# First projection of an encoder kernel: the order of casts and low parts against the latents, set by hand

## The chip, the cores and the metric

The kernel runs on 1 core of one Trainium2 chip. The metric is the device time of one execution in microseconds (us): a median over several runs of the same program. A profiled execution gives a trace beside it.

## The reference, cut to what matters

The reference is a two-layer encoder over 1024 rows of width 1024 in float32. Layer 0 mixes tokens by latent attention, layer 1 by differential attention; each layer then has a SwiGLU block, and a layer norm follows each of these parts. The change lies in the very first step of layer 0, in which the input is projected to three pieces and two of them are normalised:

```python
h = x @ w_in                                      # (1024, 1024) @ (1024, 704)
c_q, c_kv, k_rope = jnp.split(h, [384, 640], axis=-1)
c_q = _rmsnorm(c_q, g_q)                          # 384 columns
c_kv = _rmsnorm(c_kv, g_kv)                       # 256 columns
k_rope = _apply_rope(k_rope, cos, sin)            # 64 columns
```

where `_rmsnorm(x, g)` is `x * rsqrt(mean(x * x) + eps) * g` over the columns. The 704 columns that result are called the latents here. The queries, keys and values of all heads are made from them.

## The kernel before, in words

**Products in three parts.** Every float32 operand of a matmul is split into a high part, which is the operand rounded by a cast on ACT (ScalarE), and a low part, which is operand minus high part, made on DVE (VectorE) or POOL (GpSimd). A product is then three matmuls: high x high, high x low and low x high.

**The first projection.** The 1024 rows are worked on in eight row blocks of 128 (tb = 0 to 7). For each of them:

- `load_x` (line 1067) has SP (SyncE) load the block's transposed input into tile `x` (1076), ACT casts it into `xh` (1077), and DVE makes the low part `xl` (1078). There are two buffers for `x` and three each for `xh` and `xl`. So block tb's cast takes the buffer of block tb - 3, and has to wait until the last matmul that reads that block's `xh` has been done; in the same way for `xl`. Blocks 0 and 1 are loaded and cast in two pieces each.
- `project` (1111) runs 8 x 3 x 2 = 48 matmuls: for each of eight slices of 128 input columns and each of the three parts, one into PSUM tile `hq` (384 columns, line 1121) and one into `hk` (320 columns, line 1122). Blocks 0 and 1 are projected together, since the weights `wih`, `wil` are still arriving then. There are three PSUM banks for `hq` and three for `hk`, so block 3 takes those of block 0.
- `latents` (1125) makes the normalised rows `cn`: two sums of squares on ACT (lines 1128 and 1129, each an activation and a read of its accumulator), two small steps on DVE that make the variance `cve` (1131, 1132), a power on POOL that makes the scale `crs` (1134), five small DVE steps for the rotary columns (1138 to 1142), and two DVE steps that scale `hq` (1143) and `hk` (1144) into `cn`.
- `turn_c` (1147) transposes `cn` on TensorE in six blocks of 128 x 128 into PSUM tile `cp` (recorded at line 148, in the helper `tr`). ACT casts the result (1154) and DVE makes its low part (1155).

The loop at the end of the stage goes over row blocks (0, 1), 2, 3 and so on up to 7: load this block, project it, transpose the latents of the block before, make this block's latents.

**Beside it** the weights of the stage arrive in eight slices (`wraw`, cast at line 136 into `wih`, low part at line 137 into `wil`), and so do the first weights of the attention that follows (`r_wa`, cast at line 136 into `h_wa`, low part on POOL at line 137 into `l_wa`).

**What sets the order.** Each engine carries out its own instructions in the order of its queue. The order is not the order of the program's text: a planner in the framework goes through the program with a model of how long each operation takes, and gives every engine what is ready in the model. Data dependences become semaphore waits. The helper `behind(i, j)` (155) adds a dependence without a semaphore: instruction `i` keeps its place behind `j` in the plan. It is used elsewhere in the kernel before; the first projection has none. `ends` is a dictionary in which such instructions are kept for later use.

Of the kernel before, what the change touches and what calls it, by code (L numbers as in the profile page):

```python
# [11 lines left out]
AF = mybir.ActivationFunctionType  # L12
ALU = mybir.AluOpType
# [29 lines left out]
def trunk(  # L43
# [33 lines left out]
    V, A, G, T = nc.vector, nc.scalar, nc.gpsimd, nc.tensor  # L77
# [29 lines left out]
    def f32(t):  # L107
        return t.bitcast(F32)
# [4 lines left out]
    def ps_s(name):  # L113
        return ps.tile([P, 512], F32, tag="s", bufs=ps_bufs[0], name=name)

    def ps_m(name):
        return ps.tile([P, 512], F32, tag="m", bufs=ps_bufs[1], name=name)

    def ps_t(name):
        return ps.tile([P, 512], F32, tag="t", bufs=ps_bufs[2], name=name)  # L120
# [4 lines left out]
    def small(name, n=1):  # L125
        return sp.tile([P, 2], F32, tag="small", name=name, bufs=22)[:, :n]

    def load_w(src, cols, name, hi=None, lo=None, eng=None, raw=None, ins=False):

        if raw is None:  # L130
            raw = wp.tile([P, 1024], F32, tag="wr", bufs=2, name=f"r_{name}")
        nc.sync.dma_start(raw[:, :cols], src)
        if hi is None:
            hi = wp.tile([P, 1024], F32R, tag="wh", name=f"h_{name}")
            lo = wp.tile([P, 1024], F32R, tag="wl", name=f"l_{name}")
        A.copy(hi[:, :cols], raw[:, :cols])
        j = (eng or G).tensor_tensor(lo[:, :cols], raw[:, :cols], f32(hi[:, :cols]), ALU.subtract)
        return (hi, j.ins) if ins else (hi, lo)
# [8 lines left out]
    def tr(ps_out, in_):  # L147
        T.transpose(ps_out, in_, ident)

    def bcast_row(pool, src, n, name, tag):  # L150
        t = pool.tile([P, n], F32, tag=tag, name=name, bufs=1)
        nc.gpsimd.dma_start(t, src.partition_broadcast(P))
        return t

    def behind(i, j):

        tc.add_manual_dep(
            i, j.name,
            mybir.DependencyInfo(mybir.DependencyClass.NoSync, mybir.DependencyReason.DATA),
            reason="kept in program order",  # L160
        )
# [46 lines left out]
    ends = {}  # L208
# [855 lines left out]
    with tc.tile_pool(name="a0", bufs=2, side="right") as pool:  # L1064
        xs, win = {}, []

        def load_x(tb, k0=0, k1=KD):

            if tb not in xs:
                xs[tb] = [  # L1070
                    pool.tile([P, D], dt, tag=tag, name=f"{tag}_{tb}", bufs=2 if tag == "x" else 3)
                    for dt, tag in ((F32, "x"), (F32R, "xh"), (F32R, "xl"))
                ]
            c = slice(k0 * P, k1 * P)
            xt, xh, xl = (t[:, c] for t in xs[tb])
            nc.sync.dma_start(xt, xt_in[tb, :, c])
            A.copy(xh, xt)
            V.tensor_tensor(xl, xt, f32(xh), ALU.subtract)

        def load_w_in(k, n=1):  # L1080
            hi = pool.tile([P, 704], F32R, tag=f"wih{k}", name=f"wih{k}", bufs=1)
            lo = pool.tile([P, 704], F32R, tag=f"wil{k}", name=f"wil{k}", bufs=1)
            raw = pool.tile([P, 704], F32, tag="wraw", name=f"wraw{k}", bufs=5)
            win.append((hi, lo))
            if n == 1:
                _, j = load_w(w_in_a[k], 704, f"win{k}", hi, lo, G if k > 2 and k % 2 else V, raw, True)
                return j
            for c in (slice(0, 384), slice(384, 704)):
                nc.sync.dma_start(raw[:, c], w_in_a[k][:, c])
                A.copy(hi[:, c], raw[:, c])  # L1090
                V.tensor_tensor(lo[:, c], raw[:, c], f32(hi[:, c]), ALU.subtract)


        load_x(0, 0, 2)
        load_w_in(0, 2)
        load_x(1, 0, 2)
        load_w_in(1)
        load_x(0, 2, 8)
        load_w_in(2)
        load_x(1, 2, 8)  # L1100
        third = load_w_in(3)
        for k in range(4, KD):
            load_w_in(k)
        nc.sync.dma_start(ident, c_ident)
        with tc.issue_after(third):
            kt = pool.tile([P, NTB, P], F32, tag="kt", name="kt", bufs=1)
            nc.gpsimd.dma_start(kt, c_krope)
            gq = bcast_row(pool, g_q, RQ, "gq", "gq")
            gk = bcast_row(pool, g_kv, RKV, "gk", "gk")

        def project(tbs):
            ms = [(ps_m(f"hq{tb}"), ps_t(f"hk{tb}")) for tb in tbs]
            for k in range(KD):
                kc = slice(k * P, (k + 1) * P)
                wh, wl = win[k]
                for tb, (hq, hk) in zip(tbs, ms):
                    _, xh, xl = xs[tb]
                    for lh, w, st, sp_ in (
                        (xh, wh, k == 0, False), (xh, wl, False, False), (xl, wh, False, k == KD - 1)
                    ):  # L1120
                        T.matmul(hq[:, :384], lh[:, kc], w[:, 0:384], start=st, stop=sp_)  # L1121
                        T.matmul(hk[:, :320], lh[:, kc], w[:, 384:704], start=st, stop=sp_)
            return ms

        def latents(tb, hq, hk):
            junk = pool.tile([P, 384], F32, tag="junk", name=f"junk{tb}")
            ssq = small(f"ssq{tb}", 2)
            A.activation(junk, hq[:, :384], AF.Square, accum_out=ssq[:, 0:1])
            A.activation(junk[:, :256], hk[:, :256], AF.Square, accum_out=ssq[:, 1:2])
            ve = small(f"cve{tb}", 2)  # L1130
            V.tensor_scalar(ve[:, 0:1], ssq[:, 0:1], 1.0 / RQ, RMS_EPS, ALU.mult, ALU.add)
            V.tensor_scalar(ve[:, 1:2], ssq[:, 1:2], 1.0 / RKV, RMS_EPS, ALU.mult, ALU.add)
            rs = small(f"crs{tb}", 2)
            G.tensor_tensor(rs, ve, mhalf, ALU.pow)
            cn = pool.tile([P, 768], F32, tag="cn", name=f"cn{tb}")
            ra = pool.tile([P, 64], F32, tag="ra", name=f"ra{tb}")
            rb = pool.tile([P, 64], F32, tag="rb", name=f"rb{tb}")
            V.tensor_tensor(ra, hk[:, 256:320], kt[:, tb, 0:64], ALU.mult)
            V.tensor_tensor(rb[:, 0:32], hk[:, 288:320], kt[:, tb, 64:96], ALU.mult)
            V.tensor_tensor(rb[:, 32:64], hk[:, 256:288], kt[:, tb, 96:128], ALU.mult)  # L1140
            V.tensor_tensor(cn[:, 640:704], ra, rb, ALU.add)
            V.tensor_tensor(cn[:, 704:768], ra, rb, ALU.add)
            V.scalar_tensor_tensor(cn[:, :384], hq[:, :384], rs[:, 0:1], gq, ALU.mult, ALU.mult)
            V.scalar_tensor_tensor(cn[:, 384:640], hk[:, :256], rs[:, 1:2], gk, ALU.mult, ALU.mult)
            return cn

        def turn_c(tb, cn):
            hf, c, tcs = tb // 4, slice((tb % 4) * P, (tb % 4) * P + P), slice(tb * P, tb * P + P)
            for k0, nk, dst in ((0, 4, [t[hf][:, :, c] for t in lat4]), (4, 2, [t[:, :, tcs] for t in lat2])):
                pc = ps_s(f"cp{tb}_{k0}")  # L1150
                for k in range(nk):
                    tr(pc[:, k * P:(k + 1) * P], cn[:, (k0 + k) * P:(k0 + k + 1) * P])
                src = pc[:, :nk * P].rearrange("p (k t) -> p k t", k=nk)
                A.copy(dst[0], src)
                V.tensor_tensor(dst[1], src, f32(dst[0]), ALU.subtract)

        done = []
        for tbs in ((0, 1), (2,), (3,), (4,), (5,), (6,), (7,)):
            for tb in tbs:
                if tb > 1:  # L1160
                    load_x(tb)
            ms = project(tbs)
            for tb, cn in done:
                turn_c(tb, cn)
            done = [(tb, latents(tb, *m)) for tb, m in zip(tbs, ms)]
        for tb, cn in done:
            turn_c(tb, cn)
# [177 lines left out]
    with ExitStack() as st:  # L1345
# [11 lines left out]
        for ql in q_lo:  # L1357
            for mp in range(2):
                b = slice(64 - mp * 64, 128 - mp * 64)
                z = bb[b, :512]  # L1360
                i = G.tensor_tensor(ql[b, mp * 512:mp * 512 + 512], z, z, ALU.subtract).ins
# [260 lines left out]
```

## Time and profile before

| | us |
|---|---|
| median of 3 runs | 2267.78 |
| lowest and highest of them | 2267.59, 2267.83 |
| the profiled execution's own time | 2268.24 |
| its span, from the first instruction to the last | 2266.5 |

In the lines of the profile PE is TensorE's matmuls and PEld its weight loads; DVE, ACT, POOL and SP are the engines named above, and a q behind the name is the engine's queue of DMA issues. A line of a timeline has the start in us from the beginning of the span, the length, the engine, the line of the kernel, the operation, the tile written and the tiles read, the shapes, and a count where neighbours are merged. Where the engine stood still ahead of it, square brackets give how long and what ended the wait. A line of the waits says who waited for whom: us in total, how often, and the longest. Buffer numbers are left out of the tiles' names, so `xl` is the low part of any row block. Matmuls overlap, so a matmul's length is more than the time between two starts.

### The profile page before, as it was taken

Reading aid. Unit: us, or ns where it says so; the run is one execution under the profiler, and the core shown is the slowest. Engines: PE = TensorE matmul, PEld = TensorE weight load, DVE = VectorE, ACT = ScalarE, POOL = GpSimd, SP = SyncE. Lnnn points to the kernel's source line nnn. Section 1 sums busy time; section 2 is a strip of 40 time slices with the busy share of each in tenths; the row PEclk is TensorE's granted clock in tenths of the full one; section 3 lists DMA queues with packets and bytes.
Section 4 is the critical chain, followed back from the end, with each engine's and each line's share of the span. In section 5 each row is a group of like instructions: output and inputs, shape, how many; then the busy total and the mean of one; then the engine's idle time right before and its main releaser. Section 6 shows DMA issues by size and latency. Waiting matters only on the chain.

```text
span 2266.5 us, 31066 instructions
## 1 busy us (share of the span) xinstructions
PE 2240.2 (99%) x11410; PEld 1912.8 (84%) x11410; DVE 1542.9 (68%) x2894; ACT 1014.3 (45%) x2097; POOL 773.9 (34%) x626
## 2 busy tenths in 40 slices
PE   8999999999999999999999999999999999999998
PEld 8999998888888888888888898878788888888886
DVE  5676765696766667767576667576686656668778
ACT  4365564352333334444465656564442333334444
POOL 3232341114444440455432424221114444430551
PEclk9999999999999999999999999999999999999999
DMA  5010125434435338454320212063334223238443
GB/s 203 11 37 31 42 70 186 143 127 151 174 130 204 114 129 327 183 192 158 98 52 22 68 34 64 21 223 126 125 138 163 90 103 107 100 112 324 165 180 150
DMA packets 105545, 287.76 MB, mean 127 GB/s; under 512 B 7968, under 2 KB 30112, under 8 KB 94896
## 3 DMA queue, kind: packets, MB, share of 16 engines
q1 hardware_dynamic: 101552, 277.44, 34.5%
q0 software_dynamic: 3840, 8.33, 1.4%
q8 instruction: 90, 1.47, 0.3%
q14 instruction: 63, 0.52, 0.1%
HBM read 204.47 MB, written 77.07 MB: 124 GB/s over the span
## 4 chain that ended last, share of the span: by engine, by line
PE 94%; DVE 2%; DMA 1%; issue 1%; ACT 1%; POOL 0%; SPq 0%; DVEq 0%; POOLq 0%; ACTq 0%
PE gb L548 15%; PE gc L548 10%; PE ga L548 10%; PE dw L872 7%; PE dx L872 5%; PE s_a L220 4%; PE zp_a L418 3%; PE s_b L220 3%; PE dv L872 3%; PE dy L872 3%; PE bp L145 3%; PE bp L143 3%; PE bp L144 3%; PE o_a L263 2%; PE o_b L263 2%; PE hq L1121 1%
## 5 line engine op out<-in xcount | busy, mean ns | idle before, releaser
L504 ACT CAST op_g<-gr 128x512 fp32r<-128x512 f32 x240 | 146.8, 621 | 376.9 <-PE gb L548 190.6
L505 POOL TENSOR_TENSOR op_g<-gr,op_g 128x512 fp32r<-128x512 f32 x104 | 145.5, 1404 | 255.3 <-ACT op_g L504 149.5
L505 DVE TENSOR_TENSOR op_h<-rh,op_h 128x512 fp32r<-128x512 f32 x152 | 140.7, 951 | 51.5 <-ACT op_h L504 51.5
L548 PE MATMUL ga<-xh_m,op_g 128*128 128x512 f32 x512 | 168.2, 389 | 0.0
L872 PE MATMUL dw<-op_w_t,op_h 128*128 128x512 f32 x660 | 151.1, 390 | 0.0
L504 ACT CAST op_h<-rh 128x512 fp32r<-128x512 f32 x152 | 91.9, 619 | 127.2 <-PE dx L872 35.0
L872 PEld LDWEIGHTS dw<-op_w_t,op_h 128*128 128x128 f32 x660 | 123.7, 188 | 25.6
L228 ACT ACTIVATE l_b<-l_b,mx_b 128x256 f32<-128x256 f32 (+7 forms) x128 | 99.4, 777 | 73.1 <-DVE mx_b L223 71.4
L505 POOL TENSOR_TENSOR op_w_b<-rw_b,op_w_b 128x512 fp32r<-128x512 f32 x44 | 64.4, 1488 | 172.9 <-ACT op_w_b L504 165.7
L505 DVE TENSOR_TENSOR op_g<-gr,op_g 128x512 fp32r<-128x512 f32 x136 | 111.7, 825 | 16.8 <-ACT op_g L504 16.4
L872 PE MATMUL dx<-op_w_b,op_h 128*128 128x512 f32 x528 | 121.5, 390 | 1.0 <-DVE op_w_b L505 1.0
L1426 POOL TENSOR_SCALAR l_b<-l_b,rb,cst 128x128 f32<-128x128 f32 (+3 forms) x64 | 52.5, 821 | 199.3 <-DVE rb L1425 187.9
L872 PEld LDWEIGHTS dx<-op_w_b,op_h 128*128 128x128 f32 x528 | 98.8, 188 | 23.0 <-DVE op_w_b L505 2.6
L548 PE MATMUL gb<-t3h_f,op_g 128*128 128x512 f32 x352 | 115.4, 389 | 1.4 <-DVE tmp L637 1.4
L548 PE MATMUL gb<-t2h_f,op_g 128*128 128x512 f32 x352 | 115.4, 390 | 0.4 <-DVE op_g L505 0.4
L548 PE MATMUL gc<-t1h_f,op_g 128*128 128x512 f32 x352 | 115.6, 389 | 0.0
L548 PE MATMUL gb<-t4h_f,op_g 128*128 128x512 f32 x352 | 115.5, 389 | 0.0
L548 PE MATMUL gc<-b22h_f,op_g 128*128 128x512 f32 x352 | 115.3, 389 | 0.0
L548 PEld LDWEIGHTS ga<-xh_m,op_g 128*128 128x128 f32 x512 | 96.1, 188 | 19.9
L505 POOL TENSOR_TENSOR op_g<-s,op_g 128x512 fp32r<-128x512 f32 x40 | 55.3, 1381 | 167.9 <-ACT op_g L504 159.8
L143 PE MATMUL bp<-xT_f,h_wb 128*128 128x512 f32 x256 | 101.7, 397 | 0.0
L144 PE MATMUL bp<-xT_f,h_wb 128*128 128x512 f32 x256 | 101.6, 397 | 0.0
(388 smaller groups left out, 6688.6 us busy)
## 6 DMA issues: line engine op xcount, KB each, us to landing
gr<-in_w_gu SPq DMA_DIRECT2D x44, 1024.0 KB, 6.9
rh<-h_dr SPq DMA_DIRECT2D x28, 1024.0 KB, 4.9
h_dr<-sh SPq DMA_DIRECT2D x22, 1024.0 KB, 4.9
h_dr<-hp SPq DMA_DIRECT2D x22, 768.0 KB, 4.2
tt<-in_w_dn SPq DMA_DIRECT2D x22, 512.0 KB, 7.6
rh<-h_dr SPq DMA_DIRECT2D x12, 768.0 KB, 4.4
wo_dr<-op_pwo SPq DMA_DIRECT2D x16, 512.0 KB, 3.5
z<-xs_dr SPq DMA_DIRECT2D x16, 512.0 KB, 11.5
```

The costliest lines, as they stand in the source:

```text
L143: T.matmul(ps_out, lh, rh, start=(i == 0), stop=False)
L144: T.matmul(ps_out, lh, rl, start=False, stop=False)
L145: T.matmul(ps_out, ll, rh, start=False, stop=(i == n - 1))
L220: T.matmul(s[:, :w], lh, rh[:, ks], start=(j == 0), stop=(j == len(q_pass) - 1))
L228: ends["exp"] = A.activation(l[:, :n], l[:, :n], AF.Exp, bias=mx, scale=-1.0, accum_out=sm).ins
L263: T.matmul(po[:, c], a, b[:, j % 2, c], start=st, stop=sp_, skip_group_check=True)
L418: T.matmul(m, a[:, h, :], self.wo[h][w][:, c], start=(start and h == heads[0] and a is oh and w == 0), stop=(stop and h == heads[-1] and a ...
L504: turns["cast"] = A.copy(hi, src).ins
L505: return eng.tensor_tensor(lo, src, f32(hi), ALU.subtract).ins
L548: T.matmul(o, w[:, a, k * P:(k + 1) * P], x[b][:, k, :], start=(first and k == 0 and (a, b) == (0, 0)), stop=(k == 3 and a == 1), skip_gro ...
L872: T.matmul(o, h[:, a, c], w[:, b_], start=(first and (a, b_) == (0, 0)), stop=(last and a == 1), skip_group_check=True,).ins for a, b_ in ...
L1426: G.tensor_scalar(l1[:, :n], l1[:, :n], r[:, 1:2], nlam, ALU.mult, ALU.mult)
```

## The change

The cast and the low part of row blocks 3 to 7 get a fixed place in the plan: the cast of block tb comes behind the second sum of squares of block tb - 3 on ACT, and its low part behind the last step of the latents of block tb - 3 on DVE. The other lines keep the instructions concerned in `ends`. No instruction, no tile and no transfer is added or taken away.

```diff
@@ load_x
             nc.sync.dma_start(xt, xt_in[tb, :, c])
-            A.copy(xh, xt)
-            V.tensor_tensor(xl, xt, f32(xh), ALU.subtract)
+            i, j = A.copy(xh, xt).ins, V.tensor_tensor(xl, xt, f32(xh), ALU.subtract).ins
+            if tb > 2:
+                behind(i, ends["squares", tb - 3])
+                behind(j, ends["latents", tb - 3])
@@ latents
-            A.activation(junk[:, :256], hk[:, :256], AF.Square, accum_out=ssq[:, 1:2])
+            ends["squares", tb] = A.activation(junk[:, :256], hk[:, :256], AF.Square, accum_out=ssq[:, 1:2]).ins
@@ latents, at its end
-            V.scalar_tensor_tensor(cn[:, 384:640], hk[:, :256], rs[:, 1:2], gk, ALU.mult, ALU.mult)
+            ends["latents", tb] = V.scalar_tensor_tensor(
+                cn[:, 384:640], hk[:, :256], rs[:, 1:2], gk, ALU.mult, ALU.mult
+            ).ins
```

## The prediction

> **What bounds the kernel now.** I read the page first, then TensorE's waits, the timelines of DVE, ACT, POOL and PE around the one wait that the change can reach, and the table of windows there.
>
> ```profile
> span 2266.5 us, 31066 instructions
> PE 2240.2 (99%) x11410; PEld 1912.8 (84%) x11410; DVE 1542.9 (68%) x2894; ACT 1014.3 (45%) x2097; POOL 773.9 (34%) x626
> PE 94%; DVE 2%; DMA 1%; issue 1%; ACT 1%; POOL 0%; SPq 0%; DVEq 0%; POOLq 0%; ACTq 0%
> ```
>
> TensorE is busy for 99% of the span and makes up 94% of the chain that ended last. An edit on ACT and DVE can only pay where TensorE stands still or runs slowly. Its waits in the first 100 us:
>
> ```profile
> PE hq L1121 <- ACT wih L1090: 4.6, 1, 4.6
> PE cp L148 <- DVE cn L1143: 1.9, 1, 1.9
> PE s_a L220 <- ACT kn L1259: 0.4, 1, 0.4
> ```
>
> Only the second lies in the code that the change touches: the transposes of row block 0's latents (cp) wait 1.9 us for DVE's line 1143. The windows show what that wait does (columns: stretch, its length, then busy time and count of PE, PEld, DVE, ACT, POOL, the granted clock, the DMA share and GB/s):
>
> ```profile
> 30.19:33.60 3.41, 1.50 (x11) 1.20 (x10) 3.35 (x16) 1.26 (x5) 3.01 (x3) 1.00 0.83 239
> 33.60:37.01 3.41, 3.41 (x13) 3.41 (x12) 1.56 (x4) 2.00 (x5) 0.67 (x2) 0.50 0.81 297
> 37.01:40.43 3.42, 3.42 (x25) 3.39 (x24) 3.26 (x14) 0.86 (x2) 0.69 (x1) 1.00 0.53 153
> 1675.41:1678.82 3.41, 2.04 (x10) 1.41 (x9) 3.41 (x5) 0.62 (x1) 1.16 (x1) 1.00 0.00 0
> 1678.82:1682.24 3.42, 3.42 (x17) 2.79 (x16) 3.42 (x7) 1.26 (x2) 0.00 (x0) 1.00 0.00 0
> 40.43:83.95 43.52, 43.52 (x275) 42.07 (x273) 20.77 (x66) 12.07 (x35) 3.44 (x5) 1.00 0.00 1
> 83.95:85.70 1.75, 1.02 (x8) 0.82 (x7) 1.61 (x4) 1.75 (x5) 1.29 (x1) 1.00 0.00 0
> ```
>
> In the first stretch TensorE stands still for 3.41 - 1.50 = 1.91 us; in the next it is busy throughout at a granted clock of 0.50 and gets 13 matmuls done where the stretch after it has 25. So the stall is paid twice: 1.91 us of standing and 3.41 x 0.5 = 1.71 us of half speed, 3.62 us together. At 1675 us, 3.41 - 2.04 = 1.37 us of standing in as long a stretch is followed by a clock of 1.00, so I take the bound to lie between 1.37 and 1.91 us. From 40.43 to 83.95 PE has no gap: whatever is won before that moves everything behind it.
>
> **Why the stall is there.** DVE, ACT and POOL in order of time (start, length, engine, line, operation):
>
> ```profile
> 27.99 2.24 DVE L1078 TENSOR_TENSOR xl<-x,xh 128x1024 fp32r<-128x1024 f32 x1 [7.90 <-ACT xh L1077]
> 30.15 0.14 DVE L1131 TENSOR_SCALAR cve<-ssq 128x1 f32<-128x1 f32 x1
> 30.85 0.22 DVE L1142 TENSOR_TENSOR cn<-ra,rb 128x64 f32<-128x64 f32 x1
> 30.99 1.22 DVE L1078 TENSOR_TENSOR xl<-x,xh 128x1024 fp32r<-128x1024 f32 x1
> 32.12 0.61 DVE L1143 SCALAR_TENSOR_TENSOR cn<-hq,crs,gq 128x384 f32<-128x384 f32 x1
> 32.65 0.47 DVE L1144 SCALAR_TENSOR_TENSOR cn<-hk,crs,gk 128x256 f32<-128x256 f32 x1
> ```
>
> ```profile
> 26.90 1.05 ACT L1077 CAST xh<-x 128x1024 fp32r<-128x1024 f32 x1 [1.42 <-PE hk L1122]
> 27.86 0.48 ACT L1128 ACTIVATE junk<-hq 128x384 f32<-128x384 f32 x1
> 28.74 0.20 ACT L1129 ACTIVATION_READ_ACCUMULATOR junk<-hk 128x1 f32 x1
> 28.83 1.04 ACT L1077 CAST xh<-x 128x1024 fp32r<-128x1024 f32 x1
> 30.51 0.73 ACT L136 CAST h_wa<-r_wa 128x640 fp32r<-128x640 f32 x1 [0.16 <-DMA r_wa<-in_w_a]
> ```
>
> ```profile
> 25.48 3.67 POOL L137 TENSOR_TENSOR l_wa<-r_wa,h_wa 128x896 fp32r<-128x896 f32 x2
> 30.43 0.72 POOL L1134 TENSOR_TENSOR crs<-cve,cst 128x2 f32<-128x2 f32 x1 [1.28 <-DVE cve L1132]
> 31.31 2.30 POOL L137 TENSOR_TENSOR l_wa<-r_wa,h_wa 128x640 fp32r<-128x640 f32 x1 [0.16 <-ACT h_wa L136]
> ```
>
> ```profile
> 26.70 0.33 PE L1121 MATMUL hq<-wih,xl 128*128 128x384 f32 x1
> 26.87 0.31 PE L1122 MATMUL hk<-wih,xl 128*128 128x320 f32 x1
> 30.57 0.31 PE L1122 MATMUL hk<-wih,xl 128*128 128x320 f32 x1
> 32.79 0.55 PE L148 MATMUL cp<-ident,cn 128*128 128x128 f32 x3 [1.92 <-DVE cn L1143]
> 33.52 0.45 PE L1121 MATMUL hq<-wih,xl 128*128 128x384 f32 x1
> ```
>
> Block 0's projection ends at 26.87 + 0.31 = 27.18. Ahead of its squares ACT casts block 3 (xh, 1.05 us); ahead of its variances (cve, line 1131) DVE makes block 3's low part (xl, 2.24 us), and ahead of line 1143 that of block 4 (1.22 us). Line 1143 ends at 32.73; PE had run out at 30.57 + 0.31 = 30.88.
>
> **The change, step by step.** It adds and removes no instruction and no DMA. It fixes the order for blocks 3 to 7: cast behind the squares, low part behind line 1144, each of the block three before.
>
> 1. *Squares of block 0.* They no longer wait for the cast. They start with the projection's end, 27.1, and take 28.74 + 0.20 - 27.86 = 1.08 us: done at 28.2 instead of 28.94. The cast of block 3 follows at 28.1 and ends at 29.1 (if block 1's squares, about 1 us, also get in front, at 30.1), before PE's 30.88. So it costs nothing; without that cover, 1.2 us.
>
> 2. *Variances and scale.* DVE is free, so cve runs at 28.2 instead of 30.15. POOL is busy until 25.48 + 3.67 = 29.15; then crs, 0.72: done at 29.9 instead of 31.15. POOL is what is late now: the gain here is 1.25 us and not the 1.95 us of cve.
>
> 3. *Line 1143 and line 1144.* The low part of block 4 no longer stands between: 29.95 to 30.55, and 30.5 to 30.95. PE comes to the transposes at 30.88 and finds them ready. The 1.91 us go.
>
> 4. *What is late next: block 3's own low part.* It ended at 30.23; now it cannot start before line 1144 has ended. At 1.22 us (the row of 30.99, in which DVE came first and POOL's l_wa second) it ends at 30.95 + 1.22 = 32.15. PE wants it 33.52 - 32.79 = 0.73 us after the first transpose, at 31.6. That leaves 0.55 us, unless the queue has the second half of the transposes and the first hk products ahead of it, about as much again as those 0.73 us. Which order the planner gives PE the trace cannot show; I take 0.3 us, the middle of 0 and 0.55, and keep both ends.
>
> 5. *The clock.* 0.3 us of standing in that stretch is below the 1.37 us that left the clock at 1.00, so the half-speed stretch goes: 1.71 us. [...]
>
> 6. *Low part beside POOL.* The two low parts of one shape above took 2.24 and 1.22 us. In the first, POOL was inside l_wa until 29.15, and DVE finished 30.23 - 29.15 = 1.08 us after that: it was held until POOL let go. If POOL's third l_wa (31.31) starts first, the low part of step 4 waits in the same way. That is the second rival below.
>
> 7. *The other blocks and the queues.* The low parts of blocks 4 to 7 come later by the latents in front of them, at most some 3 us. Rows of the later blocks:
>
> ```profile
> 47.05 0.47 DVE L1144 SCALAR_TENSOR_TENSOR cn<-hk,crs,gk 128x256 f32<-128x256 f32 x1
> 52.75 1.22 DVE L1078 TENSOR_TENSOR xl<-x,xh 128x1024 fp32r<-128x1024 f32 x1 [1.26 <-ACT xh L1077]
> 55.44 0.48 DVE L1144 SCALAR_TENSOR_TENSOR cn<-hk,crs,gk 128x256 f32<-128x256 f32 x1
> 60.19 0.82 PE L148 MATMUL cp<-ident,cn 128*128 128x128 f32 x6
> 68.57 0.82 PE L148 MATMUL cp<-ident,cn 128*128 128x128 f32 x6
> 30.25 2.31 SPq L1076 DMA_DIRECT2D x<-in_xt  x2
> 33.64 0.33 SPq L132 DMA_DIRECT2D r_wa<-in_w_a  x1
> ```
>
> Block 7's low part (52.75) moves behind the 55.44 row, to about 57.2; block 6's behind 47.05, to 48.8. PE starts on blocks 6 and 7 behind the transposes at 60.19 and 68.57, and on block 5 one such step (8.4 us) before the first. That is 11 us of slack: cost nothing. The SP queue issues block 5's load when block 3's low part frees the buffer (30.25), now about 1.9 us later, and with it the load of block 6 and r_wa behind it; block 5 is used at 52, so this hides too.
>
> Sum: 1.91 - 0.3 + 1.71 = 3.3 us off the profiled execution's 2268.24, so 2264.9; the median of the runs, 2267.78, lies 0.46 under that execution, so **2264.5**. That is 0.15%. A measurement of this kernel can tell about 0.2%, 4.5 us, from no change, so I forecast "same", on the faster side.
>
> **The rivals.**
>
> *Latents of block 1 get in front too, clock kept.* DVE takes lines 1143 and 1144 of block 1 (about 1 us) ahead of block 3's low part, which then ends at 33.1. PE stands 33.1 - 31.6 = 1.5 us, less what it can draw forward (block 1's six transposes, 0.82 us by the rows of six above): 0.7 us. Gain 1.91 - 0.7 + 1.71 = 2.9: 2264.9; if nothing can be drawn forward and the clock still holds, 2.1: 2265.7. For it: crs of block 1 can follow right on that of block 0 on POOL. Chance 0.17.
>
> *The low part is held by POOL: the slower side.* Same place, but POOL's l_wa begins first, after its cast (30.51 + 0.73). By its columns it needs 640/896 of half of 3.67 us, 1.3 us, and by its own row 2.30; so it ends between 32.6 and 33.6, and the low part 1.08 us later, about 34.1. PE stands 34.1 - 31.6 = 2.5 us, and a half-speed stretch follows: 2.5 + 1.71 = 4.2 against 3.62, **2268.4**. It decides from a low part that ends after 31.6 + 1.91 = 33.5. Against it: in step 4 DVE starts first. Chance 0.06, a third of it with enough lost elsewhere to be slower by over 0.2%.
>
> *The half speed has another cause and stays*: only the standing time goes, 1.6 us: 2266.2. Against it: the clock falls at the end of the very stretch with the stall. Chance 0.05. [...]
>
> *The change doesn't reach the stall*: the planner, which orders all engines from a modelled timeline, puts POOL's or DVE's other work in the place that came free: 2267.8. Chance 0.05.
>
> *The planner also orders later stages anew.* TensorE's gaps of over 1 us further on show the size, 1.37 us at 1675; several such, either way. Chance 0.09: 0.05 for faster by over 0.2%, 0.02 for slower, the rest inside.
>
> My forecast has the remaining 0.58.
>
> **The numbers.** The best case is the whole 3.62 us and the 1.75 - 1.02 = 0.73 us that TensorE stands at 83.95 to 85.70: 2263.4. The upper end takes in the slower rival: 2268.4. What is left out is the re-ordering of later stages beyond this. Faster by over 0.2% needs more than 4.5 us, which only that rival gives: 0.05. Slower by over 0.2%: 0.02 of it and 0.02 of the slower rival, 0.04. Same: 0.91.
>
> **What would show it.** PE's wait for line 1143 gone from its waits, no clock of 0.50 between 33 and 37 us, line 1143 at about 30, block 3's low part behind line 1144 at 31 to 32, crs of block 0 right behind POOL's two l_wa. Wrong would be: PE waiting on xl instead, for over 1 us, or the 0.50 still there.

## The result, and the profile after

| | us |
|---|---|
| before, median of 19 runs (lowest, highest) | 2267.22 (2265.81, 2269.43) |
| after, median of 19 runs (lowest, highest) | 2263.19 (2261.99, 2265.33) |
| ratio, with its 95% interval | 0.9982 (0.9976 to 0.9988) |
| the profiled execution of after, its own time and its span | 2264.72, 2263.0 |

The change makes the kernel 4.0 us faster, 0.18%. The forecast was 3.3 us and 2264.5; the result lies 0.2 us under the low end of the range. The baseline alone is more than that: the three runs that the prediction had (2267.78) stand 0.56 us over the 19 runs made here. That 3.3 and 4.0 lie so near each other is luck all the same: the rest of this document shows two errors behind it which nearly cancel.

The head of the page of after, and below it TensorE's waits in its first 100 us (total, times, longest):

```profile
span 2263.0 us, 31059 instructions
PE 2239.2 (99%) x11410; PEld 1912.2 (84%) x11410; DVE 1545.3 (68%) x2894; ACT 1014.7 (45%) x2097; POOL 776.2 (34%) x626
```

```profile
PE hq L1123 <- ACT wih L1092: 4.7, 1, 4.7
PE hq L1123 <- ACT xh L1077: 1.2, 1, 1.2
PE s_a L220 <- ACT kn L1263: 0.4, 1, 0.4
```

The wait of the transposes (cp) for cn is gone, as forecast. But there is another one, 1.2 us for block 1's first cast, which was 0.2 us in the profile of before. The windows of after:

```profile
30.19:33.60 3.41, 3.41 (x24) 3.37 (x24) 3.24 (x13) 3.38 (x9) 0.76 (x2) 1.00 0.21 73
33.60:37.01 3.41, 3.41 (x24) 3.41 (x23) 3.38 (x10) 1.82 (x8) 2.22 (x2) 1.00 0.56 166
```

No standing and no clock of 0.50: 24 matmuls in each stretch, where before had 11 and 13. The timelines of VectorE, of GpSimd and of TensorE in after (lines from 1078 on have moved by two or more: the last two steps of the latents are 1145 and 1146 now, cast and low part are both 1077):

```profile
30.23 0.15 DVE L1134 TENSOR_SCALAR cve<-ssq 128x1 f32<-128x1 f32 x1 [0.35 <-ACT junk L1131]
...
31.22 0.62 DVE L1145 SCALAR_TENSOR_TENSOR cn<-hq,crs,gq 128x384 f32<-128x384 f32 x1
31.76 0.47 DVE L1146 SCALAR_TENSOR_TENSOR cn<-hk,crs,gk 128x256 f32<-128x256 f32 x1
32.15 1.22 DVE L1077 TENSOR_TENSOR xl<-x,xh 128x1024 fp32r<-128x1024 f32 x1
```

```profile
25.02 3.64 POOL L137 TENSOR_TENSOR l_wa<-r_wa,h_wa 128x896 fp32r<-128x896 f32 x2
30.46 0.72 POOL L1136 TENSOR_TENSOR crs<-cve,cst 128x2 f32<-128x2 f32 x1 [1.80 <-DVE cve L1134]
```

```profile
32.74 0.49 PE L148 MATMUL cp<-ident,cn 128*128 128x128 f32 x3
32.99 0.42 PE L1123 MATMUL hq<-wih,xh 128*128 128x384 f32 x1
33.24 0.34 PE L1123 MATMUL hq<-wil,xh 128*128 128x384 f32 x1
33.42 0.49 PE L148 MATMUL cp<-ident,cn 128*128 128x128 f32 x3
33.66 0.39 PE L1124 MATMUL hk<-wih,xh 128*128 128x320 f32 x1
33.89 0.30 PE L1124 MATMUL hk<-wil,xh 128*128 128x320 f32 x1
34.04 0.34 PE L1123 MATMUL hq<-wih,xl 128*128 128x384 f32 x1
```

Everything is in the order that the change asks for. Yet the first transposes stand at 32.74, where the profile of before had them at 32.79. In these two executions the stall is gone, and TensorE is no earlier at this point, because it came to the place later: its 140th matmul starts at 31.95 us in after and at 29.92 in before, behind the longer wait at 7 us and a clock that rose to 1.00 at 13.15 us instead of 9.71 (in both traces the 128x384 products take 0.53 us just ahead of that and 0.34 behind it). Counted from that matmul, the 280 up to the 420th take 43.2 us in after and 46.9 in before, so this pair of executions does win 3.7 us here. Whether others do, and what else has changed, one pair can't tell. TensorE's waits between 1600 and 1700 us, at the start of layer 1's SwiGLU, first in before, then in after:

```profile
PE gb L548 <- DVE tmp L637: 1.4, 1, 1.4
PE xTp_a L148 <- DVE z_a L184: 1.3, 1, 1.3
PE zp_a L418 <- DVE oh_a L407: 0.3, 1, 0.3
PE zp_a L418 <- ACT oh_a L406: 0.2, 1, 0.2
```

```profile
PE gb L548 <- DVE tmp L637: 1.0, 1, 1.0
PE zp_a L418 <- DVE oh_a L407: 0.3, 1, 0.3
PE zp_a L418 <- ACT oh_a L406: 0.2, 1, 0.2
```

The edges of the change are 1590 us away from this place, but the planner has ordered it anew. Before puts the transposes of a row block's normalised output (xTp_a) ahead of the second product of the first gate tile (ga); after puts that product first, and no longer waits for the layer norm (z_a). TensorE's order differs at three places in all: here, at the first projection, and at 1085 us, where the transposes behind layer 0's SwiGLU (xTp_f) meet the first value products of layer 1's attention (bv). The record of e_latefull below calls this middle place layer 0's SwiGLU.

### The profile page after: what moved, and what is told of

It reads as the page before. It is cut to its first block, busy times and chain, and to the rows that moved or that the text cites. A ratio compares the mean times of both kernels' runs of the same rounds, so it can differ in the third digit from the quotient of the medians.

```text
span 2263.0 us, 31059 instructions
## 1 busy us (share of the span) xinstructions
PE 2239.2 (99%) x11410; PEld 1912.2 (84%) x11410; DVE 1545.3 (68%) x2894; ACT 1014.7 (45%) x2097; POOL 776.2 (34%) x626
## 4 chain that ended last, share of the span: by engine, by line
PE 95%; DVE 2%; DMA 1%; issue 1%; ACT 1%; POOL 0%; SPq 0%; DVEq 0%; POOLq 0%; ACTq 0%
PE gb L548 15%; PE ga L548 10%; PE gc L548 10%; PE dw L872 7%; PE dx L872 5%; PE s_a L220 4%; PE zp_a L418 3%; PE s_b L220 3%; PE dv L872 3%; PE dy L872 3%; PE bp L145 3%; PE bp L143 3%; PE bp L144 3%; PE o_a L263 2%; PE o_b L263 2%; PE hq L1123 2%
```

## The experiments

Theory A (the first one): two gains, the larger at the first projection (the stall and its half-speed stretch, 3.6 us), the smaller, 1.3 to 1.7 us, at the re-planned place. Rival B: the later place is noise and the first projection is all. C and D ask whether the edges of blocks 4 to 7 count, and whether the half speed hangs on the stall. Each run is set against the median of before in its own set of runs. A ratio of these runs is good to about 0.0009, 2 us; differences below that are read from the profiles beside the times.

**e_early: the change, with the later place as before.** Two edges give the start of layer 1's SwiGLU the order of TensorE that it has in before:

```diff
@@ ffn of layer 1, on the change
+                if n == 0 and pr == "2":
+                    ends["gate0", layer] = made[0]
@@ transposes of the last row block
+                if ("gate0", 1) in ends and k == 3:
+                    behind(ends["gate0", 1], turned.ins)
```

> The changed kernel, with the order of before at the start of layer 1's SwiGLU (unit 0's second gate product behind the transposes of the last row block). Theory A: no stall and no clock of 0.50 in the first projection, the 1.3 us wait for line 184 near 1625 us is back, and the time is 1.3 to 1.7 us over the changed kernel, 2.3 to 3.6 us under before (ratio 0.9985 to 0.9990). Rival B: as the changed kernel, ratio 0.9982.

Measured: 2266.15 against 2266.95, ratio 0.9995 (0.9986 to 1.0004). Of the 4.0 us only 0.8 are left (by the interval, 3.2 faster to 0.9 slower) when the start of layer 1's SwiGLU is put back; the place at 1085 us keeps the order of after. TensorE's waits in e_early at the later place are those of before again:

```profile
PE xTp_a L148 <- DVE z_a L184: 1.4, 1, 1.4
PE gb L550 <- DVE tmp L641: 1.4, 1, 1.4
```

So B falls, and by these medians A has its sizes the wrong way round: the later place is the larger part.

**e_late: before, with edges that put those transposes behind the second gate product.**

```diff
@@ ffn of layer 1, on before
+                if n == 0 and pr == "2":
+                    ends["gate0", layer] = made[-1]
@@ transposes of the last row block
+                if ("gate0", 1) in ends:
+                    behind(turned.ins, ends["gate0", 1])
```

> The kernel before with one edge, far from the change: in layer 1 the transposes of the last row block come behind the gate product of unit 0's second half, as the planner happened to put them in the changed kernel. The first projection keeps the order of before. Theory A (the change has two gains: 3.6 us in the first projection, stall and half-speed stretch, and some 1.3 to 1.7 us from the re-planned start of layer 1's SwiGLU): PE's 1.3 us wait for line 184 near 1628 us is gone, the clock of 0.50 behind 33.6 us stays, and the time is 1.3 us under before (ratio 0.9994). Rival B (the wait near 1628 us differs from run to run and the order has no part in it): the wait is there or not, and the time is that of before (1.0000).

Measured: 2266.49 against 2266.95, ratio 0.9997 (0.9988 to 1.0005). This lies between A (0.9994) and B (1.0000) and decides nothing, because the edges move the transposes, but not the rest of the order, and e_late waits in other places, 1.5 us in sum:

```profile
PE ga L550 <- ACT pg L621: 0.9, 1, 0.9
PE gb L550 <- ACT op_g L506: 0.6, 1, 0.6
```

**e_latefull and e_latefull2: before, with the later order of after written out.** The order of instructions at the two later places, 1085 us and the start of layer 1's SwiGLU, is taken from after and tied together edge by edge: in e_latefull TensorE's alone, in e_latefull2 TensorE's, ScalarE's and VectorE's. The first projection stays that of before.

```diff
@@ at the end of trunk, on before
+    for runs in AFTER:
+        order = [made[f"I-{n}"] for a, b in runs for n in range(a, b)]
+        for j, i in zip(order, order[1:]):
+            behind(i, j)
```

> The kernel before, its first projection untouched, with TensorE's order at its two later places (layer 0's and layer 1's SwiGLU) written out as the kernel after has it. Theory J (most of the gain is the re-planned start of layer 1's SwiGLU): 3.0 us under the kernel before, 2264.0 us, ratio 0.9987, no wait over 0.9 us between 1600 and 1700 us. Theory A (two gains, the larger one at the first projection): 1.3 us under it, ratio 0.9994.

Measured: 2265.94 against 2267.66, ratio 0.9994 (0.9985 to 1.0003). TensorE's order by itself isn't enough: its waits in e_latefull are now for ScalarE's casts, which still come in the order of before.

```profile
PE ga L89 <- ACT pg L637: 1.0, 1, 1.0
PE ga L89 <- ACT pg L635: 0.5, 1, 0.5
```

> The kernel before, its first projection untouched, with the order of the kernel after at the two later places written out for TensorE, ScalarE and VectorE together; with TensorE's order alone, TensorE still waited 1.5 us there for a cast of ScalarE. Theory J (the re-planned start of layer 1's SwiGLU is worth 3.0 us, the first projection 0.8 us): 2.5 to 3.3 us under the kernel before, ratio 0.9985 to 0.9989, TensorE's waits between 1600 and 1700 us under 1.0 us in sum beside the 0.5 us for oh_a. Rival M (the later order is worth no more than TensorE's order alone gave, and the rest of the 4 us belongs to the first projection): 1.0 to 1.8 us under it, ratio 0.9992 to 0.9996.

Measured: 2263.84 against 2267.46, ratio 0.9984 (0.9975 to 0.9993). With three engines in the order of after, nearly the whole gain, 3.6 us (by the interval, 1.6 to 5.7), comes without any edge at the first projection. TensorE's waits between 1600 and 1700 us in e_latefull2 are down to the two for oh_a, while its wait for cn at 33 us is still there (in this kernel a helper records every instruction of the three engines, so all lines are L97; in the one before they are L89):

```profile
PE zp_a L97 <- DVE oh_a L97: 0.3, 1, 0.3
PE zp_a L97 <- ACT oh_a L97: 0.2, 1, 0.2
```

The waits are as theory J said, and the gain lies a little over its 2.5 to 3.3 us; of M's 1.0 to 1.8 us the interval holds the top alone. By e_early the start of layer 1's SwiGLU is worth 2266.15 - 2263.19 = 3.0 us, by e_latefull2 both later places together 3.6.

**b_again, b_third, a_again: why the first projection gives so little.** These are the two kernels unchanged, profiled again.

> The kernel before, unchanged, for a second profile. Theory A: a wait of 1.9 us for cn at 31 us and a window of 0.50 right behind it, as in the first. Theory G: the wait is anywhere from 1.1 to 2.0 us, and the window of 0.50 may be missing. Theory H (the wait of 1.1 us for block 1's first load, seen in the three profiles with an edge on block 3 and in none of the three without, belongs to the new order): no wait over 0.3 us at 6 us. Rival to H (it is chance): it can be there here too.

> The kernel before, unchanged, for a third profile. Theory K (block 0's latents come at a time that VectorE and GpSimd set, and TensorE's arrival varies with the start, so the wait is what is left between them): the first transposes at 32.0 to 32.9 us whatever the start, with a wait of 1.9 us where TensorE was not held up at 6 us, and 0.9 us where it was held up by over 1 us there. Theory A: a wait of 1.9 us and a window of 0.50 behind it.

> The kernel after, unchanged, for a second profile. Theory K: no wait for cn, the first transposes at 31.3 to 32.8 us, so that little is gained there against the kernel before, and no clock of 0.50 at 33 us; no wait over 0.9 us between 1600 and 1700 us. Theory A: the first transposes come 1.9 us earlier than in the kernel before.

b_again, TensorE's waits at the start:

```profile
PE hq L1121 <- ACT xh L1077: 1.2, 1, 1.2
PE cp L148 <- DVE cn L1143: 0.9, 1, 0.9
```

and its windows, in the stretches of the prediction:

```profile
30.19:33.60 3.41, 2.50 (x17) 2.21 (x16) 3.38 (x16) 2.28 (x6) 2.15 (x2) 1.00 0.70 224
33.60:37.01 3.41, 3.41 (x23) 3.37 (x22) 1.88 (x5) 2.10 (x6) 0.78 (x2) 1.00 0.77 252
```

So theory H falls (the wait of 1.2 us for block 1's first load is there without the change), the stall is 0.9 us instead of 1.9 and lies below what A and G had, and there is no stretch at half speed, which G allowed for. VectorE and GpSimd in b_again show where the other 1.0 us was:

```profile
29.10 1.22 DVE L1078 TENSOR_TENSOR xl<-x,xh 128x1024 fp32r<-128x1024 f32 x1 [8.78 <-ACT xh L1077]
31.09 1.22 DVE L1078 TENSOR_TENSOR xl<-x,xh 128x1024 fp32r<-128x1024 f32 x1
```

```profile
24.83 3.66 POOL L137 TENSOR_TENSOR l_wa<-r_wa,h_wa 128x896 fp32r<-128x896 f32 x2
```

Block 3's low part takes 1.22 us here and took 2.24 in the profile that was predicted from: there it began at 27.99, while GpSimd was in l_wa until 29.15; here it begins at 29.10, and l_wa has ended at 28.49. e_late lies between, with l_wa until 28.40:

```profile
27.97 1.51 DVE L1082 TENSOR_TENSOR xl<-x,xh 128x1024 fp32r<-128x1024 f32 x1 [7.91 <-ACT xh L1081]
```

```profile
24.73 3.67 POOL L137 TENSOR_TENSOR l_wa<-r_wa,h_wa 128x896 fp32r<-128x896 f32 x2
```

All six profiles of kernels with the first projection of before:

| | TensorE held up between 5 and 8 us | l_wa ends | block 3's low part takes | wait for cn | first transposes |
|---|---|---|---|---|---|
| before | 0.2 | 29.15 | 2.24 | 1.92 | 32.79 |
| e_late | none | 28.40 | 1.51 | 1.19 | 32.05 |
| b_again | 1.2 | 28.49 | 1.22 | 0.91 | 32.89 |
| b_third | 1.0 | 28.63 | 1.23 | 0.91 | 33.00 |
| e_latefull | 0.8 | 28.59 | 1.23 | 0.91 | 32.55 |
| e_latefull2 | 1.0 | 28.43 | 1.23 | 0.91 | 33.15 |

The wait is the low part's length less 0.32 us in every row (0.31 in one). In the four executions in which TensorE was held up early, block 3's cast and low part came later too, missed l_wa, and the stall was 0.91 us. Theory K, which had the latents at a fixed time, is wrong in its mechanism: with TensorE late the whole chain is late with it, and what changes the wait is whether the low part meets l_wa. Six profiles with block 3's low part behind block 0's latents (after, a_again, e_early, e_only3, e_cast, e_low) have no wait for cn.

The traces also give the parts of the gain apart, whatever the start of an execution took. All 14 profiles hold 11410 matmuls, and outside of the three places in one order, so the time from one number in TensorE's sequence to another can be compared (us):

| matmuls | with the order of before there | with the order of after there |
|---|---|---|
| 140th to 420th, first projection | 46.9 in before, 44.6 in e_late, 44.3 to 44.4 in b_again, b_third, e_latefull, e_latefull2 | 43.2 to 43.3 in after, a_again, e_early, e_only3, e_cast; 43.5 in e_low |
| 5400th to 5700th, at 1085 us | 43.2 in before, b_again, b_third, e_late | 43.0 in after, a_again, e_early, e_only3, e_cast, e_low, e_from4, e_latefull2 |
| 8600th to 8900th, layer 1's SwiGLU | 69.4 to 69.6 in before, b_again, b_third, e_from4, e_early | 66.4 to 67.8 in after, a_again, e_only3, e_cast, e_low; 66.2 in e_latefull2 |

Against the four executions with a stall of 0.91 us the first projection gains 1.1 us, against e_late 1.4, and against the profile that was predicted from 3.7: in the mean of these six against six 1.5 us. The place at 1085 us gives 0.2 to 0.3, the start of layer 1's SwiGLU 2.3 in the mean of these five against five. (e_late and e_latefull, with a part of the later order, take 68.3 and 68.2 us there; e_latefull takes 43.6 at 1085 us.) The sum, 4.1 us, agrees with the 4.0 that were measured; e_early's 0.8 and e_latefull2's 3.6 agree with these parts within their intervals.

**e_only3, e_from4, e_cast, e_low: which edges.** The condition or one of the edges is changed:

```diff
-            if tb > 2:
+            if tb == 3:     # e_only3
+            if tb > 3:      # e_from4
...
-                behind(j, ends["latents", tb - 3])     # left out in e_cast
-                behind(i, ends["squares", tb - 3])     # left out in e_low
```

> The two edges for row block 3 alone. Theory A says that only block 3's cast and low part stood in front of what PE waited for (with the low part of block 4, which the planner moves too): no stall behind 30.9 us, clock 1.00, ratio as the changed kernel (0.9982). Rival C (the later blocks' order matters too): up to 1 us less gain, 0.9986.

> The two edges for row blocks 4 to 7 without block 3. Block 4's low part (1.2 us) no longer stands ahead of line 1143, but block 3's does. Theory A: line 1143 starts when POOL's scale is there, at 31.2 instead of 32.1, the stall shrinks from 1.9 to 1.0 us, which is below the 1.37 us that left the clock at 1.00, so the half-speed stretch goes all the same: 2.6 us under before (0.9988). Rival D (the half speed does not come from the stall): the 0.50 stays and 0.9 us are won (0.9996).

> The change with its edges on the casts alone: block 3's low part is free to go where the planner likes, and the queue of VectorE has it behind block 0's latents by itself; the low parts of blocks 4 and 5 stand ahead of later latents again. The later stages are ordered as in the kernel after. Theory A (what counts at the first projection is block 0's latents, and the casts are what freed them): no wait for cn at 31 us, 2263.2 us, ratio 0.9982. Rival E (the low parts are what stood in the way): a wait of 1 to 2 us for cn is back, 2264.2 to 2266.5, ratio 0.9987 to 0.9997.

> The change with its edges on the low parts alone: ScalarE casts block 3 ahead of block 0's squares again (about 1 us), VectorE's order is that of the kernel after as far as block 3. The later stages are ordered as in the kernel after. Theory A, by step 2 of the prediction (GpSimd's l_wa, not the squares, decides when crs can start): crs no more than 0.3 us later, no wait for cn over 0.3 us, 2263.2 us, ratio 0.9982. Rival F (the squares decide): block 0's latents 0.7 to 1.0 us later, a wait of 0.4 to 0.8 us for cn, 2263.6 to 2264.0, ratio 0.9984 to 0.9986.

| | us | before beside it | ratio (95% interval) | wait for cn | later place ordered as in |
|---|---|---|---|---|---|
| e_only3 | 2263.05 | 2266.95 | 0.9982 (0.9974 to 0.9991) | none | after |
| e_from4 | 2265.7 | 2266.95 | 0.9996 (0.9987 to 1.0005) | 0.3 | before |
| e_cast | 2264.3 | 2267.1 | 0.9985 (0.9976 to 0.9993) | none | after |
| e_low | 2263.38 | 2267.1 | 0.9982 (0.9973 to 0.999) | none | after |

Any of the four edits takes most of the stall away, since each of the operations in front of the latents is over 0.91 us long (the cast 1.05 us, a low part 1.22) and one less is enough; the times follow the last column (e_cast lies 0.9 us over e_low, which these runs don't tell apart). Rivals C and E fall: e_only3 is as fast as after, and e_cast has no wait. e_from4 won 1.3 us, where A had 2.6 and D 0.9. That its profile has no clock of 0.50 at the first projection doesn't decide about D, since five of the six with the order of before have none either; e_delay3 below does. e_low also bears on step 2 of the prediction. Its crs:

```profile
25.20 3.68 POOL L137 TENSOR_TENSOR l_wa<-r_wa,h_wa 128x896 fp32r<-128x896 f32 x2
31.30 0.72 POOL L1135 TENSOR_TENSOR crs<-cve,cst 128x2 f32<-128x2 f32 x1 [2.42 <-DVE cve L1133]
```

With block 3's cast ahead of the squares again, crs comes 0.84 us later than in after, and GpSimd has stood for 2.42 us: the squares decide when crs starts, not l_wa, as rival F says. But no wait for cn follows, since TensorE comes to the transposes at 32.81 only; from the 140th to the 420th matmul e_low is 0.3 us longer than after.

**e_delay3: the stall brought back into after.** Three VectorE products are put ahead of block 0's latents (and one more edge, not shown, keeps the last two steps of each block's latents in order):

```diff
+            for i in range(3 if tb == 0 else 0):
+                j = V.tensor_tensor(cn[:, :640], kt8[:, :640], kt8[:, 128:768], ALU.mult).ins
+                behind(j, turned)
+                turned = j
```

> The kernel after with three VectorE products of 0.73 us each put ahead of block 0's latents, which brings the stall back while the order of the later stages stays that of the kernel after. The stall should be 1.5 to 2.6 us. Theory A (each such stall is followed by a window at half speed, 1.71 us): 2263.2 + 1.5 to 2.6 + 1.7 = 2266.4 to 2267.5, and a clock of 0.50 in the profile. Theory G (half speed follows in some executions only, so that its mean price is well under 1.71): 2264.7 to 2266.2.

Measured: 2269.95 against 2267.1, ratio 1.0009 (1.0000 to 1.0018), 6.8 us over after. The planner put block 1's latents in front as well, so the stall is 3.2 us and not the 1.5 to 2.6 expected, and the time lies over the ranges of both theories. Its windows:

```profile
32.64:36.05 3.41, 0.60 (x3) 0.54 (x4) 3.41 (x6) 1.33 (x5) 1.85 (x2) 1.00 0.14 27
36.05:39.47 3.42, 3.42 (x15) 3.16 (x15) 3.42 (x10) 0.86 (x2) 0.39 (x1) 0.50 0.50 152
```

This stall is paid twice, as step 5 had it: 3.2 us of standing and half of 3.42, 1.7 us, for the stretch at 0.50, together 4.9 us; the 140th to the 420th matmul take 48.3 us here, 5.1 more than in after. The other 2 us fit waits that after does not have, in layer 0; TensorE's waits of e_delay3 between 340 and 510 us:

```profile
PE gb L548 <- DVE tmp L637: 1.3, 1, 1.3
PE zp_a L143 <- ACT ob L1292: 1.0, 1, 1.0
```

The same view of after is empty. The order behind the first projection is that of after on TensorE, and on VectorE and ScalarE too as far as the tiles' names and shapes show it. So the trace doesn't show a new order as the cause, and why tmp and ob come later there stays open.

## Why the prediction came out as it did

- *Step 1, squares earlier: right.* They follow block 0's projection directly, and the cast of block 3 behind them cost nothing.
- *Step 2, GpSimd's l_wa sets crs: wrong.* In after l_wa ended at 28.66 and crs began at 30.46, released by cve. It made no difference to the sum.
- *Step 3, "the 1.91 us go": right in kind, mis-sized.* The wait goes, but 1.91 us was the length of one execution. It holds 1.02 us by which block 3's low part took longer beside GpSimd's l_wa (2.24 us against 1.22); 0.91 us is what four of the six profiles have. The prediction saw this (step 6) and used it for a rival, but did not take it out of the stall that it priced. What it read there is found twice more: the low part ended 1.08 us after l_wa in before (30.23 and 29.15) and in e_late (29.48 and 28.40), and block 4's 1.09 us after it in after (36.90 and 35.81). Why it does, no run shows.
- *Step 4, 0.3 us of standing for block 3's low part: it was 0.* The planner put the second half of the transposes and the first hk products ahead, as the step allowed: the low part ended at 33.37, and its first matmul came at 34.04. (The step's 30.95 + 1.22 is 32.17 and not 32.15; nothing hangs on it.)
- *Step 5, 1.71 us for the clock: there, but mis-sized as a term.* The half-speed stretch stands in one of the six profiles of the order before, behind a wait of 1.92 us. Behind 0.91 us in b_again the clock is 1.00 in both stretches; in the other four, behind 0.91 or 1.19 us, the 128x384 products at 34 us take 0.33 to 0.35 us, where those of before take 0.52. In e_delay3 the stretch behind a stall of 3.2 us has 0.50.
- *Step 7, the other blocks and the queues: right.* e_only3 has the edges of block 3 alone, and comes out the same.
- *The rival "the planner also orders later stages anew" is what happened.* It had a chance of 0.09. The prediction named the wait of 1.37 us at 1675 as the size of such a gain, but the sum and the low end of the range left it out. Two such waits in one place were there to go.

So the forecast of 3.3 us at the first projection failed in its size (0.8 us in e_early's time, 1.5 in the mean of the traces), and 2.3 us by the traces, 3.0 by e_early's time, that it hadn't counted came from a place that the change doesn't touch. What stays open is why the planner's order flips there: it flipped in after, e_only3, e_cast, e_low and e_delay3, and not in e_from4, and nothing in the code says which edit would.

## What to carry to other kernels

A stall read from one profile is one draw: before pricing it, look at what its length is made of, and take out what hangs on a chance meeting, such as a low part that runs into another engine's operation (2.24 us here, against 1.22). Where a planner orders all engines from one model, any added edge can re-order stages far behind it, so the waits that already stand there are part of the range, both those that may go and those that may come. To see what an edit did by itself, write the order of the other stages out and time the two parts apart.

## What the runs showed of the hardware

In before the granted clock is 0.50 from 33.60 to 37.01 us, for 3.41 us, behind a stretch of the same length in which TensorE stood still for 1.91 us. Such pairs of neighbouring stretches, from the windows of seven profiles:

| | stretch | TensorE stood still in it, us | clock in the next 3.41 us |
|---|---|---|---|
| e_delay3 | 32.64:36.05 | 2.81 | 0.50 |
| before | 30.19:33.60 | 1.91 | 0.50 |
| e_early | 1492.55:1495.96 | 1.40 | 0.50 |
| a_again | 1492.93:1496.34 | 1.39 | 0.50 |
| after | 1493.50:1496.91 | 1.40 | 1.00 |
| e_early | 1625.67:1629.08 | 1.39 | 1.00 |
| e_from4 | 1624.60:1628.01 | 1.38 | 1.00 |
| before | 1675.41:1678.82 | 1.37 | 1.00 |
| b_again | 30.19:33.60 | 0.91 | 1.00 |

The prediction took a bound to lie between 1.37 and 1.91 us, which was its author's estimate from the two rows of before. 1.39 and 1.40 us are found with either clock behind them, so these rows give no bound in the standing time alone, and what else decides was not shown. Both sides in e_early:

```profile
1492.55:1495.96 3.41, 2.01 (x10) 1.17 (x10) 3.41 (x10) 1.40 (x3) 1.02 (x1) 1.00 0.99 326
1495.96:1499.37 3.41, 3.41 (x14) 3.02 (x13) 2.55 (x11) 2.31 (x6) 0.78 (x1) 0.50 1.03 424
1625.67:1629.08 3.41, 2.02 (x14) 1.80 (x14) 2.66 (x5) 1.96 (x4) 0.00 (x0) 1.00 1.01 418
1629.08:1632.49 3.41, 3.41 (x17) 2.79 (x16) 3.41 (x7) 3.38 (x6) 0.00 (x0) 1.00 0.98 345
```

The standing in the first of these stretches is made of three waits of 0.2 to 0.6 us and some shorter ones, not of one gap. The same three waits stand in before (0.23, 0.59 and 0.56 us) and in after (0.25, 0.59 and 0.55), and there the clock stays at 1.00. The half speed costs little in e_early and a_again: the 8000th to the 8300th matmul take 57.0 us in e_early and 57.2 in a_again, against 56.8 to 57.1 in the other twelve, and a later wait of 0.6 to 0.9 us in those is 0.2 in these two.

The start was the other surprise. In 11 of the 14 profiles TensorE is held up for 0.8 to 1.2 us between 5 and 8 us, for block 1's first load or for the second part of the first weights, though all these kernels issue their first loads in the same order. The clock rose to 1.00 at 13.15 us in after, where the wait is 1.2 us, and at 9.71 in before, where it is 0.2. The profile that the prediction was made from is one of the three without it.
